# Where an expert's second layer stands, and how its first-layer weights are cut, in a mixture-of-experts stage on one core

## The chip, the cores and the metric

The kernel runs on one core of one Trainium2 chip. The metric is the time of one execution in microseconds (us). Engines are named as in the profile: PE is TensorE (PEld its weight loads), DVE is VectorE, ACT is ScalarE, POOL is GpSimd, SP is SyncE, which here issues the weight transfers.

## The reference

One transformer layer over 1024 tokens of width 1024: a latent attention, an RWKV mixer, and then a mixture of 32 experts of which each token takes 4. All but the last part ends at 967 us of the span and is not touched. What matters here is, for every expert e over the tokens that chose it:

```python
u = clamped_swiglu(h[idx] @ w1[e] + b1[e])    # w1[e]: 1024 x 2048, gate and linear columns interleaved
y[idx] += (u @ w2[e] + b2[e]) * gate          # w2[e]: 1024 x 1024
```

with `clamped_swiglu(hh) = g * sigmoid(1.702 g) * (l + 1)`, where g is the gate half limited to at most 7 and l the linear half limited to ±7. All tensors are float32. After the last expert the sum is added to the residual and normalized.

## The kernel before

The experts are taken by rank of their token count; a rank has a fixed number of places (`CAP`). 21 ranks have 128 places (called thin here) and 11 have 136 to 192 (wide). `order()` mixes them: thin, wide, thin, wide, and from there on thin, thin, wide, up to a thin one at the end.

**Precision.** Every float32 product is made of fp32r matmuls. `piece()` (L1378) loads 1 MB of weights (128 partitions x 2048) into a tile `w` (5 buffers), and splits it into a high part `wsh` (L205, a cast on ACT) and a rest `wsl` (L206, a subtraction on DVE), in two halves of 1024 columns each; the split pieces have 4 buffers (`SBUF`). Tokens are split in the same way: `xTh`, `xTl` for a thin expert, `xw` for a wide one (high and low side by side), and `uTh`, `uTl` for the second layer's input. `mm()` (L189) then issues three matmuls, high x high (L193), and the two mixed ones (L194, L195).

**An expert.** Eight pieces of w1 go into the first layer, four of w2 into the second.

- A thin expert's first layer, `first()` (L1462): four PSUM accumulators `acc` of 128 x 512, each of two pieces; a piece holds all 1024 rows (8 blocks of 128, `k`) and 256 columns, so a matmul writes 256 columns. After each accumulator come one ACT and three DVE instructions (L1483 to L1487), which give 256 columns of `u`; `flip()` (L1367) turns them with PE transposes and splits them to `uT`. The last quarter of `uT` is made by `late()`, which is called inside the second layer.
- A wide expert's first layer, `first_wide()` (L1509): weights are the stationary operand, the tokens stream past, and piece j gives the accumulators of gate and linear columns j. Each j is followed by L1535 to L1546 on ACT and DVE.
- The second layer, `second()` (L1413): for a wide expert the places over 128 are a second slot with matmuls of its own (L1435, L1439) on the same pieces, two pieces at a time. It ends with `y` (L1451 to L1455, DVE) and a scatter that adds `y` to DRAM (L1459, POOL).
- Between these, `load_x()` turns and splits the next expert's tokens, and `ahead()` makes the list of places and the gather for the expert after that (L1326 to L1362).

**Order.** The program is written expert by expert: first layer, tokens of the next, places of the one after, second layer. A scheduler then sets each engine's order by a modelled timeline and priorities, so instructions of neighbouring steps are interleaved; on the chip each engine runs its list in that order and waits by semaphores.

Of the kernel before, what the change touches and what calls it, by code (L numbers as in the profile page):

```python
# [19 lines left out]
P = 128  # L20
# [3 lines left out]
KD = D // P  # L24
# [3 lines left out]
NE = 32  # L28
# [73 lines left out]
def prep(a):  # L102

    f = lambda n: np.asarray(a[n])
    o = {}
    inv = (np.float32(10000.0) ** (-np.arange(0, 32, 2, dtype=np.float32) / np.float32(32))).astype(np.float32)
    invf = np.tile(np.repeat(inv, 2), 4).reshape(P, 1)
    sgn = np.tile(np.array([-1.0, 1.0], np.float32), 64).reshape(P, 1)
    o["vec"] = np.concatenate(
        [_cols(f("c")), _cols(f("emb_ln_g")), _cols(f("emb_ln_b")), _cols(f("ada_b")[0, :2048]),  # L110
         _cols(f("q_norm_g")), _cols(f("kv_norm_g")), _cols(f("mla_out_g")), _cols(f("rwkv_mu")),
         _cols(f("rwkv_k_k")), _cols(f("rwkv_k_a")), _cols(f("rwkv_r_k")), _cols(f("rwkv_gn_g")),
         _cols(f("rwkv_gn_b")), _cols(f("rwkv_a0")), _cols(f("ln1_g")), _cols(f("ln1_b")), invf, sgn], axis=1)
    o["cst"] = consts()
    o["thr"] = (np.array(CAP)[None, :] + P * np.arange(NB)[:, None]).astype(np.float32)[None]
    o["x"] = f("x")[0]
    o["pos"] = f("positions")
    aw = f("ada_w")[0]
    o["ada1"] = aw[:, :2048].reshape(KD, P, 4, 512).transpose(2, 1, 0, 3)
    o["ada2"] = aw[:, 2048:].reshape(KD, P, 8, 512).transpose(2, 1, 0, 3)  # L120
    o["adab2"] = f("ada_b")[:, 2048:]
    o["rows"] = np.stack([f(n).reshape(-1) for n in ROWS])
    w = f("w_in")[0]
    swap = np.arange(32) ^ 1
    blocks = [w[:, 0:128], w[:, 128:256], w[:, 256:384],
              np.concatenate([w[:, 384:416], w[:, 384:416][:, swap], np.zeros((D, 64), w.dtype)], axis=1)]
    blocks += [w[:, 416 + 128 * i:416 + 128 * (i + 1)] for i in range(14)]
    o["w_in"] = np.stack([b.reshape(KD, P, P).transpose(1, 0, 2) for b in blocks])
    q = f("w_uq")[0].reshape(256, NH, 96)
    rope = q[:, :, 64:].reshape(256, 256)  # L130
    rsw = q[:, :, 64:][:, :, swap].reshape(256, 256)
    q = np.concatenate([q[:, :, :64].reshape(256, 512), rope, rsw], axis=1)
    o["w_uq"] = q.reshape(2, P, 1024).transpose(1, 0, 2)
    o["w_uk"] = f("w_uk")[0]
    o["w_uv"] = f("w_uv")[0]
    o["w2a"] = np.concatenate([f("rwkv_w2")[0], f("rwkv_w0")], axis=0)
    o["a2"] = f("rwkv_a2")[0]
    o["g2"] = f("rwkv_g2")[0]
    o["w_o"] = f("w_o")[0].reshape(KD, P, D).transpose(1, 0, 2)
    o["rw"] = f("router_w")[0].reshape(KD, P, NE).transpose(1, 0, 2)  # L140
    o["rb"] = f("router_b")

    w1 = f("exp_w1")[0].reshape(NE, KD, P, 8, P, 2)
    o["w1"] = w1.transpose(0, 3, 2, 1, 5, 4).reshape(NE, 8, P, KD, 256)
    o["w2"] = f("exp_w2")[0].reshape(NE, 4, 2, P, D).transpose(0, 1, 3, 2, 4)
    b1 = f("exp_b1")[0].reshape(NE, 8, P, 2).transpose(0, 1, 3, 2)

    o["b1r"] = np.concatenate([b1.reshape(NE, 4, 512)] * 2, axis=1)
    o["b2"] = f("exp_b2")[0]
    o["b1c"] = b1.reshape(NE, 16, P).transpose(0, 2, 1)  # L150
    return {k: np.ascontiguousarray(v) for k, v in o.items()}
# [12 lines left out]
class Build:  # L164
# [1297 lines left out]
    def first(self, e, xT):  # L1462

        nc, mp, pm = self.nc, self.mo, self.pm
        V, S, G = nc.vector, nc.scalar, nc.gpsimd
        w1 = self.i["w1"]
        bs = self.biases(e)
        u = mp.tile([P, D], F32, name="u")
        uT = self.split_tile(mp, [P, KD, P], "uT")
        for q in range(4):  # L1470
            acc = pm.tile([P, 512], F32, name="acc", bufs=4)
            nc.tensor.matmul(acc, self.pick[:, q:q + 1].to_broadcast([P, P]), bs, start=True, stop=False)
            for j in range(2):
                ws = self.piece(w1[bass.ds(e, 1), 2 * q + j].rearrange("o p k n -> (o p) (k n)"))
                for k in range(KD):
                    w, c = ws[k // 4], k % 4 * 256
                    self.mm(acc[:, j * 256:(j + 1) * 256], xT[:, k], w[:, c:c + 256],
                            start=False, stop=(j == 1 and k == KD - 1))
            with self.tc.high_priority():
                a = acc.rearrange("p (j g f) -> p j g f", j=2, g=2)  # L1480
                v2 = lambda t: t.rearrange("p (j f) -> p j f", j=2)
                sg = mp.tile([P, 256], F32, name="sg")
                S.activation(v2(sg), a[:, :, 0], AF.Sigmoid, scale=1.702)  # L1483
                ln = mp.tile([P, 256], F32, name="ln")
                V.tensor_scalar(v2(ln), a[:, :, 1], 8.0, -6.0, ALU.min, ALU.max)
                V.scalar_tensor_tensor(v2(ln), a[:, :, 0], 7.0, v2(ln), ALU.min, ALU.mult)
                V.scalar_tensor_tensor(u[:, q * 256:(q + 1) * 256], sg, SIG7, ln, ALU.min, ALU.mult)  # L1487
                if q:
                    self.flip(uT, u, 2 * q - 2, 2 * q)

        def late():
            with self.tc.high_priority():
                self.flip(uT, u, 6, 8)
        return [uT], late
# [14 lines left out]
    def first_wide(self, e, xw, slots):  # L1509

        nc, mp, pm = self.nc, self.mo, self.pm
        V, S, G = nc.vector, nc.scalar, nc.gpsimd
        cap = xw.shape[3]
        bc = mp.tile([P, 16], F32, name="bc")
        nc.sync.dma_start(bc, self.i["b1c"][bass.ds(e, 1)].rearrange("o p n -> (o p) n"))
        lin = bc.rearrange("p (j g) -> p j g", g=2)[:, :, 1]
        G.tensor_scalar(lin, lin, 1.0, None, ALU.add)
        u0 = self.split_tile(mp, [P, KD, P], "uT")
        u1 = self.u1
        n1 = cap - P  # L1520
        w1 = self.i["w1"]
        for j in range(KD):
            ws = self.piece(w1[bass.ds(e, 1), j].rearrange("o p k n -> (o p) (k n)"))
            parts = []
            for g in range(2):
                acc = pm.tile([P, 512], F32, name="acc", bufs=4)
                for k in range(KD):
                    w = ws[k // 4]
                    c = slice(k % 4 * 256 + g * P, k % 4 * 256 + (g + 1) * P)
                    nc.tensor.matmul(acc[:, 0:2 * cap], w.hi[:, c], xw[:, k].rearrange("p a t -> p (a t)"),  # L1530
                                     start=(k == 0), stop=False)
                    nc.tensor.matmul(acc[:, 0:cap], w.lo[:, c], xw[:, k, 0], start=False, stop=(k == KD - 1))  # L1532
                with self.tc.high_priority():
                    t = mp.tile([P, cap], F32, name=f"t{g}")
                    S.activation(t, acc[:, cap:2 * cap], AF.Identity, bias=bc[:, 2 * j + g:2 * j + g + 1])  # L1535
                    V.tensor_tensor(t, acc[:, 0:cap], t, ALU.add)  # L1536
                    parts.append(t)
            with self.tc.high_priority():
                gl, ln = parts
                sg = mp.tile([P, 256], F32, name="sg")[:, 0:cap]  # L1540
                S.activation(sg, gl, AF.Sigmoid, scale=1.702)
                V.tensor_scalar(ln, ln, 8.0, -6.0, ALU.min, ALU.max)
                V.scalar_tensor_tensor(ln, gl, 7.0, ln, ALU.min, ALU.mult)
                V.scalar_tensor_tensor(ln, sg, SIG7, ln, ALU.min, ALU.mult)
                self.split(u0[:, j], ln[:, 0:P])
                self.split(Split(u1[:, j, 0, 0:n1], u1[:, j, 1, 0:n1]), ln[:, P:cap])  # L1546
        return [u0, u1], None
# [84 lines left out]
    def moe(self):  # L1632
# [11 lines left out]
        slots, rows, x = {}, {}, {}  # L1644
# [7 lines left out]
        ahead(0)  # L1652
        x[0] = self.load_x(rows[0])
        ahead(1)
        for i, r in enumerate(order):
            e = nc.values_load(self.eid[0:1, r:r + 1], engines=[mybir.EngineType.SP], skip_runtime_bounds_check_because=ok)
            uT, late = self.first(e, x[i]) if len(slots[i]) == 1 else self.first_wide(e, x[i], slots[i])
            if i + 1 < NE:
                x[i + 1] = self.load_x(rows[i + 1])
            ahead(i + 2)  # L1660
            self.second(e, slots[i], uT, late, i == NE - 1)

    def overflow(self):

# [144 lines left out]
```

## Time and profile before

| | |
|---|---|
| time, median of 3 runs | 2460.11 us (2459.35 to 2463.05) |
| the profiled execution: its time / its span | 2454.54 us / 2452.8 us |
| busy over the span: PE, DVE, ACT, POOL | 2280.2, 2003.6, 1409.0, 562.3 us |
| expert stage, from about 967 to 2400 us: its length / DVE busy / ACT busy | 1433.0 / 1297.42 / 970.52 us |
| weights loaded in it | 384 pieces of 1024 KB |

A matmul's busy time in the trace is longer than the time until the next one can start, since matmuls are pipelined; what a matmul takes of PE is read from start to start. PE's granted clock is a share of full speed (1.00 is 2.4 GHz, 0.50 is 1.2 GHz).

### The profile page before, as it was taken

The numbers are of one execution on the slowest core, as the hardware profiler recorded it, in microseconds if no ns is written. First come the engines' busy times: TensorE is split into PE (matmuls) and PEld (weight loads), VectorE is DVE, ScalarE is ACT, GpSimd is POOL, SyncE is SP. The second block draws the span as 40 slices with busy tenths as digits, with TensorE's granted clock in tenths as the row PEclk, the third lists the DMA queues.
The fourth block names the chain that finished last, engine by engine and source line by source line (L and its number), as shares of the span: only waits on it lengthen the run. The fifth ranks groups of instructions, "written<-read, shape, count | busy, mean of one in ns | idle before, by whom it ended". The sixth has DMA issues, their size and how long they took to land. (4 is left out here: it accounts for less than half of the span.)

```text
span 2452.8 us, 42049 instructions
## 1 busy us (share of the span) xinstructions
PE 2280.2 (93%) x15539; PEld 1934.8 (79%) x15539; DVE 2003.6 (82%) x3878; ACT 1409.0 (57%) x2355; POOL 562.3 (23%) x411
## 2 busy tenths in 40 slices
PE   6999989999998995999999999999999999999992
PEld 3776766776665784889898998989999898888881
DVE  7666447778786776789898989898989899898977
ACT  5323325455555433667676767676767676666764
POOL 1004223222213433111111312121312121221113
PEclk9999989999999996899999999999999999999996
DMA  6377542222123323878798989797989898898973
GB/s 269 119 257 275 199 113 56 58 46 58 33 42 85 113 94 140 313 282 311 290 341 297 329 288 348 276 356 275 350 287 343 308 327 321 297 330 301 325 271 138
DMA packets 167334, 567.80 MB, mean 231 GB/s; under 512 B 64616, under 2 KB 79737, under 8 KB 116820
## 3 DMA queue, kind: packets, MB, share of 16 engines
q1 hardware_dynamic: 155476, 524.63, 58.6%
q0 software_dynamic: 11216, 39.34, 6.5%
q8 instruction: 124, 2.03, 0.3%
q10 hardware_dynamic: 432, 1.09, 0.1%
q14 instruction: 86, 0.70, 0.1%
HBM read 508.22 MB, written 56.79 MB: 230 GB/s over the span
## 5 line engine op out<-in xcount | busy, mean ns | idle before, releaser
L206 DVE TENSOR_TENSOR wsl<-w,wsh 128x1024 fp32r<-128x1024 f32 x786 | 935.9, 1224 | 138.4 <-ACT wsh L205 136.9
L205 ACT CAST wsh<-w 128x1024 fp32r<-128x1024 f32 x786 | 782.8, 1047 | 345.2 <-PE acc L195 91.1
L193 PE MATMUL acc<-wsh,xTh 128*128 128x256 f32 x1344 | 382.4, 286 | 9.9 <-ACT xTh L205 6.2
L194 PE MATMUL acc<-wsl,xTh 128*128 128x256 f32 x1344 | 383.3, 286 | 0.7 <-DVE wsl L206 0.7
L1530 PE MATMUL acc<-xw,wsh 128*128 128x368 f32 (+7 forms) x1408 | 376.8, 351 | 6.0 <-DVE t L1536 6.0
L195 PE MATMUL acc<-wsh,xTl 128*128 128x256 f32 x1344 | 382.1, 285 | 0.3 <-DVE xTl L206 0.3
L1532 PE MATMUL acc<-xw,wsl 128*128 128x184 f32 (+7 forms) x1408 | 335.9, 239 | 0.0
L1530 PEld LDWEIGHTS acc<-xw,wsh 128*128 128x128 f32 x1408 | 265.9, 189 | 7.9 <-issue 3.2
L1532 PEld LDWEIGHTS acc<-xw,wsl 128*128 128x128 f32 x1408 | 270.3, 192 | 0.7
L193 PEld LDWEIGHTS acc<-wsh,xTh 128*128 128x128 f32 x1344 | 258.9, 193 | 13.3 <-ACT xTh L205 8.4
L194 PEld LDWEIGHTS acc<-wsl,xTh 128*128 128x128 f32 x1344 | 259.8, 193 | 4.8 <-DVE wsl L206 1.0
L195 PEld LDWEIGHTS acc<-wsh,xTl 128*128 128x128 f32 x1344 | 259.6, 193 | 1.7 <-DVE xTl L206 0.6
L1459 POOL DMA_INDIRECT y_d<-y,idx x42 | 148.4, 3532 | 403.2 <-DVE y L1451 318.6
L1362 POOL DMA_INDIRECT xg<-h_d,idx x43 | 99.1, 2305 | 614.7 <-issue 267.8
L193 PE MATMUL acc<-wsh,uTh 128*128 128x512 f32 x512 | 203.3, 400 | 18.0 <-ACT uTh L205 18.0
L194 PE MATMUL acc<-wsl,uTh 128*128 128x512 f32 x512 | 202.4, 396 | 0.0
L195 PE MATMUL acc<-wsh,uTl 128*128 128x512 f32 x512 | 192.7, 404 | 1.2 <-DVE uTl L206 1.2
L193 PEld LDWEIGHTS acc<-wsh,uTh 128*128 128x128 f32 x512 | 97.4, 190 | 39.9 <-ACT uTh L205 20.8
L193 PE MATMUL sm<-hTh,wsh 128*128 128x512 f32 x288 | 116.2, 404 | 7.2 <-DVE stage L445 2.2
L194 PE MATMUL sm<-hTl,wsh 128*128 128x512 f32 x288 | 116.9, 406 | 4.2 <-DVE hTl L347 3.1
L195 PE MATMUL sm<-hTh,wsl 128*128 128x512 f32 x288 | 114.9, 399 | 0.0
L194 PEld LDWEIGHTS acc<-wsl,uTh 128*128 128x128 f32 x512 | 97.6, 191 | 19.2
(584 smaller groups left out, 4337.2 us busy)
## 6 DMA issues: line engine op xcount, KB each, us to landing
w<-in_w_dram SPq DMA_DIRECT2D x384, 1024.0 KB
aw<-in_ada_dram SPq DMA_DIRECT2D x34, 512.0 KB
w<-in_w_in_dram SPq DMA_DIRECT2D x18, 512.0 KB
aw<-in_ada_dram SPq DMA_DIRECT2D x7, 1024.0 KB
rkv_d<-stage SPq DMA_DIRECT2D x12, 512.0 KB
xt<-in_x_dram SPq DMA_DIRECT2D x8, 512.0 KB
xr<-in_x_dram SPq DMA_DIRECT2D x8, 512.0 KB
xr_d<-xr SPq DMA_DIRECT2D x8, 512.0 KB
```

Of the source, the lines that this page charges most:

```text
L193: mm(out, a.hi, b.hi, start=start, stop=False)
L194: mm(out, a.hi, b.lo, start=False, stop=False)
L195: mm(out, a.lo, b.hi, start=False, stop=stop)
L205: (hi_eng or self.nc.scalar.copy)(dst.hi, src)
L206: (lo_eng or self.nc.vector).tensor_tensor(dst.lo, src, dst.hi.bitcast(F32), ALU.subtract)
L1362: self.nc.gpsimd.indirect_dma_start(out=xg[0:n], out_offset=None, in_=self.h2_d, in_offset=bass.IndirectOffsetOnAxis(ap=idx[0:n, 0:1], axi ...
L1459: nc.gpsimd.indirect_dma_start(out=self.y_d, out_offset=bass.IndirectOffsetOnAxis(ap=idx[0:n, 0:1], axis=0), in_=y[0:n], in_offset=None, c ...
L1530: nc.tensor.matmul(acc[:, 0:2 * cap], w.hi[:, c], xw[:, k].rearrange("p a t -> p (a t)"), start=(k == 0), stop=False)
L1532: nc.tensor.matmul(acc[:, 0:cap], w.lo[:, c], xw[:, k, 0], start=False, stop=(k == KD - 1))
```

## The change

The host's layout of w1 is cut differently: a piece now holds 512 rows (4 blocks k) and 512 columns instead of 1024 rows and 256 columns. It is as large as before, and there are as many. In `first()` the two pieces of an accumulator are two halves of the rows, and a matmul writes all 512 columns. In `first_wide()` two pieces are loaded at every even j and serve j and j + 1. In `moe()` the second layer of an expert is issued after the next expert's first layer; for the last expert the one before it is finished first. `late` of the newer expert is handed to the older one's second layer, where a wide expert calls it once in each of its two slots.

```diff
-    w1 = f("exp_w1")[0].reshape(NE, KD, P, 8, P, 2)
-    o["w1"] = w1.transpose(0, 3, 2, 1, 5, 4).reshape(NE, 8, P, KD, 256)
+    w1 = f("exp_w1")[0].reshape(NE, 2, 4, P, 4, 2, P, 2)
+    o["w1"] = w1.transpose(0, 4, 1, 3, 2, 5, 7, 6).reshape(NE, 8, P, 4, 512)
...
-            for j in range(2):
-                ws = self.piece(w1[bass.ds(e, 1), 2 * q + j].rearrange("o p k n -> (o p) (k n)"))
-                for k in range(KD):
-                    w, c = ws[k // 4], k % 4 * 256
-                    self.mm(acc[:, j * 256:(j + 1) * 256], xT[:, k], w[:, c:c + 256],
-                            start=False, stop=(j == 1 and k == KD - 1))
+            for m in range(2):
+                ws = self.piece(w1[bass.ds(e, 1), 2 * q + m].rearrange("o p k n -> (o p) (k n)"))
+                for k in range(4):
+                    c = k % 2 * 512
+                    self.mm(acc, xT[:, 4 * m + k], ws[k // 2][:, c:c + 512], start=False, stop=(m == 1 and k == 3))
...
-            ws = self.piece(w1[bass.ds(e, 1), j].rearrange("o p k n -> (o p) (k n)"))
+            if j % 2 == 0:
+                ws = []
+                for m in range(2):
+                    ws += self.piece(w1[bass.ds(e, 1), j + m].rearrange("o p k n -> (o p) (k n)"))
...
+        due = None
         for i, r in enumerate(order):
+            last = i == NE - 1
+            if last:
+                self.second(*due, None)
             e = nc.values_load(...)
             uT, late = self.first(e, x[i]) if len(slots[i]) == 1 else self.first_wide(e, x[i], slots[i])
-            if i + 1 < NE:
+            if not last:
                 x[i + 1] = self.load_x(rows[i + 1])
-            ahead(i + 2)
-            self.second(e, slots[i], uT, late, i == NE - 1)
+                ahead(i + 2)
+                if due:
+                    self.second(*due, late)
+                elif late:
+                    late()
+            due = e, slots[i], uT
+        self.second(*due, late, True)
```

PE before, at the end of a thin expert's second layer (`uT`) ahead of the wide expert with 176 places, whose first layer reads `xw`:

```order
L1374 MATMUL tr<-csts,u 128x128 x2
L1374 MATMUL tr<-csts,xg 128x128 x8
L1374 MATMUL tr<-csts,xg 128x48 x4
L195 MATMUL acc<-wsh,uTl 128x512 x2
L193 MATMUL acc<-wsh,uTh 128x512
L194 MATMUL acc<-wsl,uTh 128x512
L195 MATMUL acc<-wsh,uTl 128x512
L193 MATMUL acc<-wsh,uTh 128x512
```

PE of the change at the same place; what follows is the rest of the 8 matmuls of L1330, two more transposes of `u`, and then the wide expert's first matmul:

```order
L193 MATMUL acc<-wsh,uTh 128x512 x2
L194 MATMUL acc<-wsl,uTh 128x512
L195 MATMUL acc<-wsh,uTl 128x512
L194 MATMUL acc<-wsl,uTh 128x512
L195 MATMUL acc<-wsh,uTl 128x512
L1374 MATMUL tr<-csts,u 128x128 x2
L1374 MATMUL tr<-csts,xg 128x128 x8
L1374 MATMUL tr<-csts,xg 128x48 x8
L1330 LDWEIGHTS oh
```

Before, some 20 matmuls of the second layer stand behind the first transposes of the wide expert's tokens (`xg`); in the change all of the second layer stands ahead of all 16. This is so at nine of the eleven wide experts, and at the first one with a first layer in place of the second.

DVE before, at the same expert, from the last thin-expert work to the split of `xw`:

```order
L206 TENSOR_TENSOR wsl<-w,wsh 128x1024 x2
L206 TENSOR_TENSOR uTl<-tr,uTh 128x256
L1486 SCALAR_TENSOR_TENSOR ln<-acc,ln 128x256
L206 TENSOR_TENSOR xw<-tr,xw 128x4x128 x2
L206 TENSOR_TENSOR xw<-tr,xw 128x4x48
L1487 SCALAR_TENSOR_TENSOR u<-sg,ln 128x256
L206 TENSOR_TENSOR wsl<-w,wsh 128x1024 x2
L206 TENSOR_TENSOR xw<-tr,xw 128x4x48
```

DVE of the change, at the same place:

```order
L1451 SCALAR_TENSOR_TENSOR y<-acc,gate,g2p 128x512 x2
L206 TENSOR_TENSOR wsl<-w,wsh 128x1024
L1486 SCALAR_TENSOR_TENSOR u<-sg,ln 128x256
L206 TENSOR_TENSOR wsl<-w,wsh 128x1024
L206 TENSOR_TENSOR uTl<-tr,uTh 128x256
L206 TENSOR_TENSOR xw<-tr,xw 128x4x128 x2
L206 TENSOR_TENSOR xw<-tr,xw 128x4x48
L1338 TENSOR_SCALAR at<-tr,csts 128x1
```

Before, `y` of the thin expert (L1451) stands 14 rows behind the first split of `xw`; in the change it stands ahead of it, with two halves of a weight piece, `u` and `uTl` between them.

## Rows read from the trace of the kernel before

**Rows 1.** Windows: start:end, us, busy us (instructions) by engine, PEclk, DMA share, GB/s.

```profile
1317.00:1448.70 131.70, 130.61 (x906) 120.32 (x905) 122.56 (x195) 90.39 (x139) 28.87 (x9) 1.00 0.87 314
```

**Rows 2.** Windows of its parts: thin first, second; thin first, second, rest; wide.

```profile
1317.00:1340.90 23.90, 23.90 (x198) 23.75 (x197) 23.90 (x30) 18.24 (x23) 7.00 (x1) 1.00 0.94 333
1340.90:1352.90 12.00, 11.37 (x70) 9.19 (x69) 12.00 (x19) 7.77 (x11) 0.00 (x0) 1.00 0.95 382
1352.90:1379.30 26.40, 26.40 (x209) 25.76 (x208) 25.74 (x35) 19.41 (x23) 12.07 (x3) 1.00 0.86 303
1379.30:1391.00 11.70, 11.24 (x66) 8.66 (x65) 11.70 (x17) 8.27 (x14) 3.30 (x1) 1.00 1.01 422
1391.00:1398.40 7.40, 7.40 (x53) 6.92 (x50) 6.66 (x12) 5.21 (x8) 1.05 (x1) 1.00 0.89 337
1398.40:1430.00 31.60, 31.60 (x242) 31.58 (x240) 29.36 (x63) 22.05 (x46) 2.50 (x1) 1.00 0.87 287
1430.00:1448.70 18.70, 18.70 (x88) 14.45 (x85) 13.21 (x24) 9.44 (x16) 2.95 (x2) 1.00 0.62 229
```

**Rows 3.** Waits of PE, 960 to 2390 us: us in total, times, longest.

```profile
PE acc L193 <- ACT uTh L205: 10.4, 9, 2.3
PE acc L193 <- ACT xTh L205: 6.2, 10, 0.6
PE acc L1530 <- DVE t L1536: 6.0, 7, 1.5
```

**Rows 4.** Waits of DVE and ACT in the same stretch.

```profile
DVE wsl L206 <- ACT wsh L205: 107.8, 99, 5.2
ACT wsh L205 <- PE acc L195: 91.1, 100, 2.1
ACT wsh L205 <- DMA w<-in_w_dram: 24.9, 14, 5.7
```

**Rows 5.** Groups by form: one of three equal lines of the thin first layer.

```profile
L193 PE MATMUL acc<-wsh,xTh 128*128 128x256 f32 x1344 | 382.4, 286 | 9.9 <-ACT xTh L205 6.2 <-ACT wsh L205 3.7
```

**Rows 6.** Timeline of PE, first into second layer: start, us, instruction [idle before].

```profile
1378.74 0.28 PE L194 MATMUL acc<-wsl,xTh 128*128 128x256 f32 x1
1379.22 0.28 PE L195 MATMUL acc<-wsh,xTl 128*128 128x256 f32 x1
...
1380.72 0.39 PE L193 MATMUL acc<-wsh,uTh 128*128 128x512 f32 x1
...
1382.09 0.38 PE L1374 MATMUL tr<-csts,u 128*128 128x128 f32 x2
1382.93 0.50 PE L193 MATMUL acc<-wsh,uTh 128*128 128x512 f32 x1 [0.46 <-ACT uTh L205]
```

**Rows 7.** Timeline of PE: twelve transposes of tokens and what follows.

```profile
1017.96 1.43 PE L1374 MATMUL tr<-csts,xg 128*128 128x128 f32 x12
1019.31 0.50 PE L194 MATMUL acc<-wsl,uTh 128*128 128x512 f32 x1
```

**Rows 8.** Timeline of DVE around a thin expert's output `y`.

```profile
1363.84 1.22 DVE L206 TENSOR_TENSOR wsl<-w,wsh 128x1024 fp32r<-128x1024 f32 x1
1364.97 1.41 DVE L1451 SCALAR_TENSOR_TENSOR y<-acc,gate,g2p 128x512 f32<-128x512 f32 x2
1366.29 2.35 DVE L206 TENSOR_TENSOR wsl<-w,wsh 128x1024 fp32r<-128x1024 f32 x2
1368.56 0.42 DVE L1487 SCALAR_TENSOR_TENSOR u<-sg,ln 128x256 f32<-128x256 f32 x1
1368.89 1.23 DVE L206 TENSOR_TENSOR wsl<-w,wsh 128x1024 fp32r<-128x1024 f32 x1
```

**Rows 9.** Groups of DVE by form, 1317 to 1448.7 us.

```profile
L206 DVE TENSOR_TENSOR uTl<-tr,uTh 128x256 fp32r<-128x256 f32 x8 | 3.4, 422 | 0.0
L206 DVE TENSOR_TENSOR xw<-tr,xw 128x512 fp32r<-128x512 f32 x2 | 1.3, 696 | 0.0
L206 DVE TENSOR_TENSOR xw<-tr,xw 128x192 fp32r<-128x192 f32 x2 | 0.7, 360 | 0.0
```

**Rows 10.** Timeline of DVE in a wide second layer.

```profile
1440.52 4.63 DVE L206 TENSOR_TENSOR wsl<-w,wsh 128x1024 fp32r<-128x1024 f32 x4 [3.49 <-ACT wsh L205]
1447.87 2.36 DVE L206 TENSOR_TENSOR wsl<-w,wsh 128x1024 fp32r<-128x1024 f32 x2 [1.40 <-ACT wsh L205]
```

More of the change, by code (lines that the diff above doesn't have):

```diff
@@ L1526, in first_wide @@
                 acc = pm.tile([P, 512], F32, name="acc", bufs=4)
+                a = j % 2 * 2 + g
                 for k in range(KD):
-                    w = ws[k // 4]
-                    c = slice(k % 4 * 256 + g * P, k % 4 * 256 + (g + 1) * P)
+                    w, c = ws[k // 2], slice(k % 2 * 512 + a * P, k % 2 * 512 + (a + 1) * P)
                     nc.tensor.matmul(acc[:, 0:2 * cap], w.hi[:, c], xw[:, k].rearrange("p a t -> p (a t)"),
```

## The prediction

> **What bounds the kernel now.** I read the windows of the expert stage first, then the waits of PE, DVE and ACT, then the timelines for what one instruction really takes. One round of the steady pattern thin, thin, wide is 131.7 us, and in it PE is busy for 130.6, DVE for 122.6, ACT for 90.4 [rows 1]. So PE sets the pace and DVE is 9.1 us behind it, with ACT and the DMA engines (0.87 of their time) further off. The parts of the round [rows 2] show that this is two different limits: over both thin experts, 1317.0 to 1391.0 us, DVE is busy for 73.3 of 74.0 us while PE is nearly full too, and the whole slack of DVE lies with the wide expert: 0.7 + 2.2 + 5.5 us in the last three windows. What ends DVE's idle time is the cast on ACT, 107.8 us in all, and what ends the waits of that cast is mostly PE letting a split buffer go (91.1 us for one of the matmul lines; weights that had not landed: 24.9 us) [rows 4]. DVE is thus held by PE's use of the four split buffers, and PE itself hardly waits: its waits for data in the steady stretch are 10.4, 6.2 and 6.0 us over the whole of it [rows 3]. What the change takes from PE counts, as far as DVE can follow.
>
> **Part 1: wider matmuls in the thin first layer.** There are 3 x 1344 matmuls of 256 columns, so 192 for each of 21 thin experts [rows 5]; 96 of 512 columns take their place. From start to start a 256-column matmul takes 0.48/4 = 0.120 us, a 512-column one of the second layer (1.37 us for six) 0.228 us [rows 6]. 192 x 0.120 = 23.04 us becomes 96 x 0.228 = 21.89 us: 1.15 us less for each thin expert, 24 us for 21. With the reading accuracy of those starts, 0.226 to 0.230, it is 20 to 28. PE's clock is at 1.00 through all of this [rows 1], so it gives nothing more. Pieces have the same bytes, number and order of arrival, so loading is unchanged; splitting too.
>
> Here a rule speaks against the change. The rows show that a matmul takes 13 ns (256 columns) and 15 ns (512) beyond its columns at 2.4 GHz: 120 against 106.7 ns, 228 against 213.3 [rows 6]. The Trainium skill, "TensorE: Matmul & The Clock Gate", section "Wait — 56ns, not 53.3ns?", gives a warm matmul its columns at 2.4 GHz plus some 2.5 ns; by that, an estimate from its figures, the halved count would save 0.25 us of a thin expert and 5 us in all instead of 24. The trace disagrees with it for these two shapes, and the sum goes by the trace.
>
> **Part 2: the second layer one expert later.** The 10.4 us that PE waits for `uTh` (9 times) stand where the second layer starts on its own expert's last quarter of `u`; rows 6 show one, with the two transposes of `u`, then 0.46 us idle, ahead of the next matmul. A first layer now lies between, so they go: -10.4. The 6.2 us for `xTh` (10 times) are at the start of a thin first layer [rows 3]; in the new order those transposes stand among the wide expert's second-layer matmuls, so I count -6.2. Bounds: from none of these to all, 0 to -16.6; I take all, since no PE instruction behind them needs the result within a microsecond.
>
> `late` runs twice in the second layer of ten wide experts: two transposes (0.24 us by the rate in rows 7), one cast and one `uTl` of 0.42 us [rows 9] too many. On PE that is +2.4 us; on DVE 4.2 us over the stage, hidden under its slack of 9.1 us a round, or added if that is gone.
>
> **Part 3: a new wait, which the order shows.** At nine wide experts all 16 transposes of `xw` now follow the whole second layer of the thin expert, and nothing but 4 transposes of `u` and 8 very short matmuls stands between them and the wide expert's first matmul, which needs `xw` split. On DVE that split is queued behind `y`, and `y` cannot start until the second layer's last matmul has ended. So from that end DVE does: `y`, 1.32 us; two halves of a piece, 2.27; `u`, 0.33, all from start to start [rows 8]; `uTl` 0.42; three splits of `xw`, 0.70 + 0.70 + 0.36 [rows 9]: 6.10 us. In this time PE has its 20 transposes, (1.35/12) x 20 = 2.25 us [rows 7]. It waits 3.85 us, nine times: +35 us. Queued behind the waiting matmul is the whole wide first layer, and DVE's sums `t` wait for it. Before, some 20 matmuls of 0.228 us, 4.6 us, covered that chain. From below: if DVE had only the splits left, 1.76 us and the cast ahead of the first, the transposes would cover it, 0; nearest to the order is 2 us as a low case, since `y` alone must come after. From above: DVE is busy without a pause in the thin experts [rows 2], so it can reach `y` late by the two halves queued ahead of it, 2.3 us more: 6.2 us each, +56. I take 3.85.
>
> **Part 4: pieces in pairs in the wide first layer.** Two pieces now serve j and j + 1 and go free together, so two of four split buffers are in use rather than one. What this does is seen where pairs are used already, in the wide second layer: DVE stops there for 3.49 and 1.40 us until a pair goes free [rows 10], with no wait of PE for it. The wide first layer has DVE at 29.4 of 31.6 us [rows 2], so PE could wait there by the second half of a pair. Against that, the pause of part 3 lets DVE get ahead at the very start of it, and the 6.0 us for `acc` [rows 3] may go. I count -4, between -6 and +20 (half of such a 3.5 us stop at each of 11 experts).
>
> **Sum.** -24 - 16.6 + 2.4 + 35 - 4 = -7.2 us on the profiled execution's 2454.5, so 2447.3. That execution was 5.6 us below the median of the three runs, 2460.1; set against the median the forecast is **2453 us**. Startup, until the clock and the transfers are up, and the last expert, whose second layer still follows its own first layer, are left as they are.
>
> **The rivals.**
> - *DVE comes late (slower).* Place: `y` ahead of `xw` at the end of the thin pair. PE gets through two thin experts 2.3 us sooner, DVE does not: it was busy for 73.3 of 74.0 us there. If it reaches `y` more than about 1 us after the second layer's end, the pause is 5 to 6.2 us and eats all gains: nine times 2.3 more is +21, so 2474. For: rows 2. Against: DVE's slack of 7.7 us in the wide expert can be spent as a lead of two to three pieces before the thin ones.
> - *The pause is short (clearly faster).* If DVE and ACT serve `xw` early enough that PE waits 2 us rather than 3.85, the sum gains 17 us: 2436. For: 20 transposes and the casts run in that time anyway. Against: the fixed order on DVE.
> - *The columns cost what they cost (slower).* If the 512-column matmuls in a stream of alternating weights save only 0.25 us of an expert, 19 us of part 1 are missing: 2472. Against: both durations are measured in this trace, among the same kind of weight loads. This is the skill's rule above.
> - That the change does not do what it says is no case: the order shows both parts.
>
> **How the numbers follow.** Forecast, 2442 to 2462: 0.42. Short pause, around 2436: 0.23. DVE late, 2462 to 2485: 0.27. The page's rule: 0.03. Anything else, slower for the most part: 0.05. 0.2% of the time, about what a measurement of this kernel can tell from no change, is 4.9 us: 2455.2 to 2465.0. Of the forecast's 0.42 some 0.25 lies below that and 0.17 within; with the short pause, faster is 0.48; the lower end of the late DVE gives the rest of the same, 0.22; slower 0.30. Eight times in ten it should lie between 2432 and 2478: the low end is the short pause with part 1 at 28 us, the high end the late DVE with a little for the pairs. The likeliest case's own range is 2442 to 2462.
>
> **What would show it.** Right: the three matmul lines of the thin first layer count 672 each, at 512 columns, 0.228 us apart; the wait of the second layer for `uTh` is gone but for the last expert; and PE has a new wait for `xw`, nine or ten times, around 4 us each, released by DVE's split. A round is then within 1 us of 131.7. Wrong: no such wait (then it is clearly faster), or one of over 5 us with DVE busy ahead of it (then slower), or new waits of PE for `wsh` or `wsl` of the second piece of a pair inside the wide first layer.

## The result, and the profile after

| | before | after |
|---|---|---|
| time, median of 6 runs each | 2460.12 us (2451.47 to 2463.05) | 2485.07 us (2476.01 to 2492.52) |
| ratio | | 1.0113, 95% interval 1.009 to 1.0135 |
| profiled execution: its time / its span | 2454.54 / 2452.8 us | 2482.1 / 2480.3 us |

The change makes the kernel 1.1% slower. To compare kernels I use one stretch throughout: from the first matmul of the second wide expert to that of the tenth, eight rounds of thin, thin, wide. In the windows view (columns as in [rows 1]) it is, in the kernel before,

```profile
1124.20:2178.10 1053.90, 1036.72 (x7235) 953.67 (x7234) 972.69 (x1555) 723.46 (x1105) 219.24 (x72) 1.00 0.87 314
```

and in the changed kernel,

```profile
1116.80:2193.20 1076.40, 1029.97 (x5713) 888.14 (x5712) 977.67 (x1572) 733.61 (x1119) 265.85 (x73) 0.97 0.84 310
```

Here lie 22.5 of the 27.5 us by which the span grew. PE is busy for 6.8 us less and idle for 29 us more, and its mean clock fell from 1.00 to 0.97: the stretches recorded at 1.2 GHz sum up to 56 us in these rounds, 3 before. DVE's busy time hardly moved. The next table divides a round of PE's time by what it runs, each matmul counted from its start to the next start, and idle times over 0.15 us taken out. The last three columns are experiments told below.

| us in a round | before | after | cut alone (e1) | cut alone, DVE lighter (e12) | after, tokens earlier (e11) |
|---|---|---|---|---|---|
| thin first layers | 46.44 | 43.76 | 44.08 | 44.24 | 43.79 |
| wide first layer | 33.90 | 35.31 | 33.78 | 33.74 | 34.78 |
| second layers | 41.36 | 41.31 | 42.96 | 41.07 | 40.86 |
| transposes, places, biases | 7.89 | 8.43 | 8.26 | 7.46 | 8.36 |
| idle | 2.15 | 5.74 | 5.03 | 0.08 | 1.70 |
| sum | 131.74 | 134.55 | 134.11 | 126.58 | 129.49 |
| at 1.2 GHz | 0.4 | 7.0 | 3.4 | 0.0 | 1.7 |

The thin first layers got shorter as forecast; idle time and a longer wide first layer took that back twice over. The new matmuls, by form (line, shape, count, busy us, mean ns), where [rows 5] had 1344 of 256 columns:

```profile
L193 PE MATMUL acc<-wsh,xTh 128*128 128x512 f32 x672 | 262.0, 394 | 6.4 <-ACT wsh L205 5.6 <-ACT xTh L205 0.7
```

What PE waits for in the changed kernel, over the stretch of [rows 3] (us in total, times, longest):

```profile
PE tr L1374 <- DVE uTl L206: 41.8, 9, 4.9
PE tr L1374 <- DVE u L1486: 9.3, 5, 7.1
PE tr L1374 <- DVE xw L206: 2.5, 9, 0.6
PE acc L1533 <- DVE xw L206: 2.2, 1, 2.2
PE acc L193 <- ACT xTh L205: 0.7, 1, 0.7
```

The waits for `uTh` are gone, those for `xTh` nearly so. New is a wait of a transpose (L1374), 51.1 us in all. Nine idle times of 4.75 to 7.11 us stand ahead of nine wide experts. This is the one at 2054 us, on PE (start, us, instruction, idle before):

```profile
2052.14 0.39 PE L195 MATMUL acc<-wsh,uTl 128*128 128x512 f32 x1
2052.84 0.44 PE L1374 MATMUL tr<-csts,u 128*128 128x128 f32 x2 [0.30 <-DVE u L1486]
2053.11 1.39 PE L1374 MATMUL tr<-csts,xg 128*128 128x128 f32 x12
2059.36 0.60 PE L1374 MATMUL tr<-csts,xg 16*128 16x16 f32 x4 [4.87 <-DVE uTl L206]
2059.96 0.35 PE L1330 MATMUL tr<-td,oh 128*128 128x6 bf16 x8
2060.56 0.69 PE L1374 MATMUL tr<-csts,u 128*128 128x128 f32 x2 [0.25 <-DVE xw L206]
2060.90 0.59 PE L1533 MATMUL acc<-xw,wsh 128*128 128x288 f32 x1
2061.28 0.32 PE L1535 MATMUL acc<-xw,wsl 128*128 128x144 f32 x1
2061.40 0.53 PE L1533 MATMUL acc<-xw,wsh 128*128 128x288 f32 x1
```

and on DVE:

```profile
2052.71 2.34 DVE L206 TENSOR_TENSOR wsl<-w,wsh 128x1024 fp32r<-128x1024 f32 x2
2054.98 1.39 DVE L1451 SCALAR_TENSOR_TENSOR y<-acc,gate,g2p 128x512 f32<-128x512 f32 x2
2056.30 2.34 DVE L206 TENSOR_TENSOR wsl<-w,wsh 128x1024 fp32r<-128x1024 f32 x2
2058.57 0.41 DVE L1486 SCALAR_TENSOR_TENSOR u<-sg,ln 128x256 f32<-128x256 f32 x1
2058.90 0.41 DVE L206 TENSOR_TENSOR uTl<-tr,uTh 128x256 fp32r<-128x256 f32 x1
2059.24 1.53 DVE L206 TENSOR_TENSOR xw<-tr,xw 128x512 fp32r<-128x512 f32 x4
```

Read them together. The second layer's last matmul starts at 2052.14. PE turns two blocks of `u` and three groups of `xw` tokens; these four results fill the four `tr` buffers. The fourth group of four transposes needs a buffer back, and the oldest is let go by `uTl` on DVE. `uTl` stands behind two halves of weights, `y`, two more halves and `u`: DVE reaches `y` only 2.8 us after that last matmul began (2.0 to 2.9 at the nine), since it is late itself. The buffer settles where PE waits, but hardly how long: DVE is through with `xw` at 2060.77, 0.13 us ahead of the wide expert's first matmul.

A stop of DVE itself shows 47 us earlier:

```profile
2007.21 0.42 DVE L206 TENSOR_TENSOR uTl<-tr,uTh 128x256 fp32r<-128x256 f32 x1 [3.64 <-ACT uTh L205]
```

DVE stands for 3.64 us, since the cast to `uTh` waits for two transposes of `u` (its third quarter), and these stand in PE's order among the matmuls of the wide expert's second layer. From there to `y` DVE has no pause over 0.22 us. Such a stop of DVE, of 3.64 to 4.90 us, comes ahead of each of the nine stops of PE; from 960 to 2390 us DVE waits 40.3 us for `uTh`, 6.5 in the kernel before. It is longer than the time by which DVE is late at `y`. Whether DVE would be in time without it, no run tells by itself.

PE stands for 4.87 us, and the clock falls to half within it and stays there behind it. In the stretch around another of these stops, at 1386 us,

```profile
1386.10:1392.90 6.80, 4.81 (x28) 4.63 (x29) 5.29 (x12) 0.69 (x2) 3.89 (x2) 0.50 0.91 310
```

the granted clock is 0.50, and PE is busy for 4.81 of the 6.80 us. A pair of wide matmuls takes 0.50 us behind the stop shown above (2060.90 to 2061.40), against 0.24 at full clock (in e11, below).

### The profile page after: what moved, and what is told of

Same layout as the page of the kernel before. It is cut to its first block, busy times and chain, and to the rows that moved or that the text cites. A ratio compares the mean times of both kernels' runs of the same rounds, so it can differ in the third digit from the quotient of the medians.

```text
span 2480.3 us, 38054 instructions
## 1 busy us (share of the span) xinstructions
PE 2275.0 (92%) x13543; PEld 1850.6 (75%) x13543; DVE 1992.6 (80%) x3888; ACT 1416.5 (57%) x2365; POOL 631.4 (25%) x411
## 5 line engine op out<-in xcount | busy, mean ns | idle before, releaser
L206 DVE TENSOR_TENSOR wsl<-w,wsh 128x1024 fp32r<-128x1024 f32 x786 | 926.4, 1218 | 73.9 <-ACT wsh L205 73.7
L1533 PE MATMUL acc<-xw,wsh 128*128 128x368 f32 (+7 forms) x1408 | 392.1, 363 | 2.2 <-DVE xw L206 2.2
L1459 POOL DMA_INDIRECT y_d<-y,idx x42 | 207.2, 4932 | 466.4 <-DVE y L1451 343.2
L1533 PEld LDWEIGHTS acc<-xw,wsh 128*128 128x128 f32 x1408 | 278.0, 198 | 2.7 <-DVE xw L206 2.5
L194 PE MATMUL acc<-wsl,xTh 128*128 128x512 f32 x672 | 265.7, 395 | 3.2 <-DVE wsl L206 3.2
L193 PE MATMUL acc<-wsh,xTh 128*128 128x512 f32 x672 | 262.0, 394 | 6.4 <-ACT wsh L205 5.6
L195 PE MATMUL acc<-wsh,xTl 128*128 128x512 f32 x672 | 264.0, 393 | 0.0
L1362 POOL DMA_INDIRECT xg<-h_d,idx x43 | 78.3, 1821 | 566.6 <-PE acc L1535 178.2
L193 PE MATMUL acc<-wsh,uTh 128*128 128x512 f32 x512 | 184.5, 401 | 6.3 <-ACT uTh L205 6.1
L193 PEld LDWEIGHTS acc<-wsh,xTh 128*128 128x128 f32 x672 | 127.8, 190 | 33.7 <-ACT wsh L205 5.9
L194 PEld LDWEIGHTS acc<-wsl,xTh 128*128 128x128 f32 x672 | 127.8, 190 | 31.0 <-DVE wsl L206 4.1
L195 PEld LDWEIGHTS acc<-wsh,xTl 128*128 128x128 f32 x672 | 127.6, 190 | 27.0 <-DVE xTl L206 0.2
L1538 ACT ACTIVATE t<-acc,bc 128x152 f32<-128x152 f32 (+7 forms) x176 | 65.4, 394 | 96.5 <-PE acc L1535 84.1
```

The lines of the kernel that those rows point to most:

```text
L193: mm(out, a.hi, b.hi, start=start, stop=False)
L194: mm(out, a.hi, b.lo, start=False, stop=False)
L195: mm(out, a.lo, b.hi, start=False, stop=stop)
L206: (lo_eng or self.nc.vector).tensor_tensor(dst.lo, src, dst.hi.bitcast(F32), ALU.subtract)
L1362: self.nc.gpsimd.indirect_dma_start(out=xg[0:n], out_offset=None, in_=self.h2_d, in_offset=bass.IndirectOffsetOnAxis(ap=idx[0:n, 0:1], axi ...
L1459: nc.gpsimd.indirect_dma_start(out=self.y_d, out_offset=bass.IndirectOffsetOnAxis(ap=idx[0:n, 0:1], axis=0), in_=y[0:n], in_offset=None, c ...
```

## The experiments

All times are medians; ratios are against runs of the kernel before on the same chip, with 95% intervals. "Cut" is the new shape of the pieces, "shift" the second layer one expert later. Theory A says that the stops ahead of the wide experts, and the clock behind them, are the loss (A', for short, that these come of the order of the `tr` buffers, whatever DVE's load); B, that pieces taken in pairs are; C, that DVE is too late whatever PE saves. Rows of waits below are of 1115 to 2330 us. Few of the forecasts came out: by the time alone B's in e1, the second of e4, C's in e10, that of A' in e11 and the second of e14; every other range was missed. So the theories are judged by the waits and the rounds, and not by the time alone.

**e1: the cut alone.** The loop of before with the new pieces:

```diff
-            due = e, slots[i], uT
-        self.second(*due, late, True)
+            ahead(i + 2)
+            self.second(e, slots[i], uT, late, i == NE - 1)
```

> The new cut of the first-layer weights alone, with the second layer where the kernel before has it. Theory A (the loss is the stop of PE ahead of a wide expert and the low clock behind it, both made by the shift): faster than before by 15 to 25 us, 2435 to 2445; the 512-column matmuls keep their pitch of 0.227, no stop of 5 us ahead of the wide experts, the uTh waits of about 20 us stay, and half-clock time in the expert stage stays near 27 us. Theory B (taking two pieces at a time in a wide first layer costs): slower than before, 2465 or more, with waits of PE for wsh or wsl at line 1533. Theory C (VectorE sets the pace, whatever PE saves): within 5 us of 2460.

Measured: 2475.82 us, ratio 1.0085 (1.0056 to 1.0115). Theory A's forecast is refuted: the cut alone loses, with no shift and no stop of 5 us. The time lies in B's range, and C's (within 5 us of 2460) is missed as well. PE waits in the thin second layers for what DVE and ACT make of `u`; at 2012 us the timeline reads

```profile
2008.89 0.69 PE L1374 MATMUL tr<-csts,u 128*128 128x128 f32 x4
2011.45 0.50 PE L193 MATMUL acc<-wsh,uTh 128*128 128x512 f32 x1 [1.87 <-ACT uTh L205]
...
2014.35 1.22 PE L195 MATMUL acc<-wsh,uTl 128*128 128x512 f32 x2 [1.70 <-DVE uTl L206]
```

In all there are 46 us of it, with no wait for `wsh` or `wsl` at L1533, which B asked for, so B has only its time:

```profile
PE acc L193 <- ACT uTh L205: 20.4, 17, 1.9
PE acc L195 <- DVE uTl L206: 11.8, 9, 1.7
PE tr L1330 <- DVE uTl L206: 10.6, 9, 1.2
PE tr L1374 <- DVE uTl L206: 3.6, 10, 0.4
```

**e2: the shift alone.** The new loop with the pieces of before.

> The second layer one expert later alone, with the first-layer pieces of before (1024 rows by 256 columns). Theory A: the nine or ten stops of about 5 us (some 52 us) and some 70 us more at half clock (worth some 34) come, less the 17 us of waits that the shift removes: slower than before by 50 to 75 us, 2510 to 2535. Theory B (the pieces taken in pairs cost): no slower than before, 2440 to 2460. Theory C (VectorE sets the pace): within 10 us of the changed kernel's 2485.

Measured: 2503.67 us, ratio 1.019 (1.0151 to 1.0228). The stops are there:

```profile
PE tr L1374 <- DVE uTl L206: 15.9, 5, 4.0
PE tr L1374 <- DVE u L1487: 14.3, 3, 5.9
```

Each half of the change loses by itself, 21 and 49 us over the kernel before on that chip (2454.83), and together they lose less than the shift alone. The 2503.67 lies in no theory's range; A's is nearest.

**e3: tokens a whole first layer earlier.**

```diff
+            if i and not last:
+                x[i + 1] = self.load_x(rows[i + 1])
...
             uT, late = self.first(e, x[i]) if len(slots[i]) == 1 else self.first_wide(e, x[i], slots[i])
```

> The changed kernel with one statement moved: the tokens of the next expert are transposed and split (load_x) ahead of the current expert's first layer, so that xw is there long before the wide expert begins. Theory A: the stop ahead of each wide expert goes (9 times about 5.5 us, 50 us) and with it the half-clock stretches behind it (some 69 us of them, worth 34): 2400 to 2425. Theory B (pairs of pieces): the stops go but PE waits for wsh or wsl in wide experts: 2455 to 2480. Theory C (VectorE sets the pace, 122 us busy in a round of 135): the stop turns up elsewhere, 2440 to 2460.

Measured: 2487.15 us, ratio 1.0136 (1.0089 to 1.0183). The stop turned up elsewhere: the tokens had not landed (PE waits 34.5 us for `xg` in ten times, 8.4 at most). So the run says nothing on the stop's price; e11 mends it.

**e4: PE kept busy in the stop.** Ahead of the fourth group of `xw`:

```diff
+                for k in range(40 if q == 0 else 0):
+                    self.nc.tensor.transpose(pt[:, 256 + k % 2 * P:384 + k % 2 * P], rows[0][:, k % 8 * P:k % 8 * P + P],
+                                             self.ident)
```

> The changed kernel with 40 needless transposes (128 by 128, about 0.117 us each, 4.7 us in all) put on PE into the unused half of a PSUM buffer at the place where it stops ahead of a wide expert, so that the stop stays as long as it is but PE isn't idle in it. If the low clock comes of PE standing still there: half-clock time in the expert stage falls from about 96 us to about 30, and the time by some 30 us, to 2450 to 2460, with the round near 131. If the low clock has another cause (load, not the stop): no half-clock time saved, 2480 to 2495.

Measured: 2483.25 us, ratio 1.0105 (1.0062 to 1.0148). The place now reads

```profile
2063.69 4.59 PE L1515 MATMUL tr<-csts,xg 128*128 128x128 f32 x40
2068.63 0.42 PE L1512 MATMUL tr<-csts,xg 16*128 16x16 f32 x4 [0.35 <-DVE uTl L206]
```

and the time at 1.2 GHz in the eight rounds went from 56 to 17 us: the low clock does come of the standing PE. Of the nine rounds to the eleventh wide expert seven have every stop filled and nothing at 1.2 GHz. Their mean is 131.65 us, against 133.64 for the same rounds of the changed kernel with 7.3 us each at 1.2 GHz: 2.0 us a round is what the clock costs. The whole time didn't fall: in the other two rounds PE stops for `u` first (8.8 and 7.1 us, from 1249 and 1792 us), the needless transposes come behind that stop, and these rounds are 9.6 and 3.6 us longer than in the changed kernel, which has the second of these stops too. My 2450 to 2460 was a miss.

The Trainium skill, "TensorE: Matmul & The Clock Gate", section "Terms", prices throttled time at one minus the share of clock granted, so at half of it. By that rule, as an estimate from it, the 7.3 us a round would cost 3.7. The runs show 2.0, less than the rule's. PE is idle in 2.0 of the 7.3 us, which explains a part of the difference.

**e5 and e6: the cut for thin experts only**, the weights lying in memory in both shapes; e5 with the loop of before, e6 with the new one.

```diff
-        w1 = self.i["w1"]
+        w1 = self.i["w1w"]
...
+            ws = self.piece(w1[bass.ds(e, 1), j].rearrange("o p k n -> (o p) (k n)"))
```

> The loop of before; the first-layer weights lie in memory in both cuts, thin experts take pieces of 512 rows by 512 columns, wide ones those of 1024 by 256 as before, so that no pieces are taken in pairs. Theory B (the pairs let VectorE run only two pieces ahead in the wide first layer, and what it doesn't do there it lacks later): faster than the 2476 of the pieces alone and than before, 2430 to 2445. Theory C (VectorE's 122 us of work in a round set the pace, and whatever PE saves in thin experts comes back as waits for u or for split pieces): 2452 to 2470.

> The changed kernel with wide experts taking pieces of 1024 rows by 256 columns (weights in memory in both cuts): the shift and the thin cut without the pairs. Theory B (pairs): VectorE's idle time in the wide first layer (6.5 us in a round of the changed kernel) shrinks to some 2 and the time falls by 20 to 40, to 2445 to 2465. Theory A (the stop by the order of the tr buffers): the stop stays, 2478 to 2490. Theory C: within 10 of 2485 too, VectorE's busy time 122 us a round and its idle time 12.

Measured: e5 2491.88 us, ratio 1.0129 (1.008 to 1.0177); e6 2498.16 us, 1.0141 (1.0099 to 1.0183). Both miss all their ranges. Without pairs neither kernel is faster than with them, so theory B has nothing for it, here or in the waits of e1. That e5 is slower than e1 is not explained; the order on each engine is planned anew for every kernel.

**e7 and e8: GpSimd takes two low half splits of each thin expert**, in the changed kernel and in the one before.

```diff
-            self.split(ws[:, slice(*c)], w[:, slice(*c)])
+            self.split(ws[:, slice(*c)], w[:, slice(*c)], lo_eng=nc.gpsimd if pool and c[0] else None)
```

> The changed kernel with two of the 24 half splits of the low part (128 by 1024, 1.13 us each on VectorE) of each thin expert done by GpSimd instead. This takes 21 x 2 x 1.13 = 47 us of VectorE's work away and none of PE's. Theory C (VectorE sets the pace): faster by 30 to 47, 2438 to 2455, VectorE's busy time in a round 117.5 instead of 122. Theory A or B alone (the stop ahead of wide experts, the pairs): it shortens the stop by the VectorE work ahead of it at most, 10 to 20 us, 2465 to 2475.

> The kernel before with the same two half splits of each thin expert on GpSimd. Theory C: faster by 20 to 47 than before, 2410 to 2435. If PE sets the pace in the kernel before, as the prediction had it (PE busy 130.6 of 131.7 us): only the 24 us of PE's waits for uTh, xTh and t can go, 2436 at best, and 2450 is likelier; slower if GpSimd's splits (2.6 to 3.9 us each, behind a scatter) come late.

Measured: e7 2476.04 us, ratio 1.0052 (1.0023 to 1.0081); e8 2506.09 us, 1.0165 (1.0123 to 1.0208). Neither is in a range. Inconclusive for C, as DVE's work did not shrink: its busy time in the eight rounds rose from 977.7 to 994.9 us in e7. The timeline shows why, on GpSimd

```profile
2105.28 2.41 POOL L206 TENSOR_TENSOR wsl<-w,wsh 128x1024 fp32r<-128x1024 f32 x1 [19.14 <-DVE t L1546]
2113.74 2.69 POOL L206 TENSOR_TENSOR wsl<-w,wsh 128x1024 fp32r<-128x1024 f32 x1 [3.47 <-ACT wsh L205]
```

and on DVE in the same time:

```profile
2105.80 2.97 DVE L206 TENSOR_TENSOR wsl<-w,wsh 128x1024 fp32r<-128x1024 f32 x1
2114.41 3.10 DVE L206 TENSOR_TENSOR wsl<-w,wsh 128x1024 fp32r<-128x1024 f32 x1
2118.55 1.22 DVE L206 TENSOR_TENSOR wsl<-w,wsh 128x1024 fp32r<-128x1024 f32 x1
```

A split on DVE takes 1.22 us by itself and about 3 beside one on GpSimd; both times it ends 1.08 us after GpSimd's. The Trainium skill, "GPSIMD Engine Reference", section "Key points", says that the two engines share SBUF interfaces and contend where a DVE instruction has two SBUF inputs, as this subtraction has; the trace agrees.

**e9, e10 and e12: a part of DVE's work left out.** Two low half splits of each thin expert are left out (PE reads another half's low part, so the output differs): e9 in the changed kernel, e10 in the one before, e12 in the cut alone.

```diff
+            if cut and c[0]:
+                nc.scalar.copy(ws.hi[:, slice(*c)], w[:, slice(*c)])
+            else:
+                self.split(ws[:, slice(*c)], w[:, slice(*c)])
+        return ws[:, 0:1024], Split(ws.hi[:, 1024:2048], ws.lo[:, 0:1024]) if cut else ws[:, 1024:2048]
```

> The changed kernel, in which two of the 24 low half splits of each thin expert are left out (PE reads another half's low part in their place, so the output differs); no engine gets other work for it. 4.5 us of VectorE's work in a round go, 47 us in all, and none of PE's. Theory C (VectorE's work and the waits that hang on it set the pace): VectorE busy about 117.5 us in a round, the stop ahead of wide experts shortens or goes, 2438 to 2455. Theory A' (the stop comes of the order of the tr buffers, whatever VectorE's load): the stop keeps over 4 us of its 4.9, 2475 to 2485.

> The kernel before with the same two low half splits of each thin expert left out (the output differs). Theory C: the 16.7 us of waits for uTh and more go, 2415 to 2440. If PE sets the pace in the kernel before and VectorE doesn't: 2445 to 2462, since PE's 130.6 us of a round's 131.7 stay.

> The new cut alone (loop of before) with two of the 24 low half splits of each thin expert left out (the output differs). If the new cut alone is slow because VectorE comes late with u and its split parts in thin experts, whose PE work got shorter: its waits for uTh, uTl and in the slots' place (44 us) shrink to under 15, a round takes 129 to 130, and the time is 2410 to 2435. If it is slow for another reason (pairs, order of the instructions): a round stays over 132.5, 2455 to 2475.

Measured: e9 2428.15 us, ratio 0.9884 (0.985 to 0.9918); e10 2436.41 us, 0.991 (0.9883 to 0.9937); e12 2401.37 us, 0.9775 (0.9753 to 0.9797). The same 47 us of DVE's work are worth 57 us in the changed kernel, 74 in the cut alone, and some 20 in the kernel before. That puts e10 into C's range, but only 2.8 of its 20 us lie in its eight rounds (1051.10 us), and most of the rest behind the tenth wide expert; PE's time without idle is 129.9 us a round there, against 129.6. e9 and e12 came out below their ranges. In e12 the eight rounds are

```profile
1130.10:2142.70 1012.60, 1011.87 (x5698) 869.90 (x5696) 934.66 (x1521) 725.04 (x1105) 170.78 (x72) 1.00 0.87 326
```

with PE busy throughout, its clock at 1.00, and as its only wait 0.9 us for `uTl`. PE needs 126.5 us for a round of the new cut, if DVE is in time.

The place where DVE's work binds is the thin pair, from its first matmul to the wide expert's. The mean of the eight pairs (windows view):

| us in a thin pair | before | before, DVE lighter (e10) | cut alone (e1) | cut alone, DVE lighter (e12) |
|---|---|---|---|---|
| length | 75.0 | 74.1 | 77.7 | 70.3 |
| DVE busy | 73.6 | 70.0 | 73.7 | 69.2 |

Two single pairs, that of the waits of e1 shown above and the same one in e12:

```profile
1986.40:2064.90 78.50, 72.44 (x349) 58.34 (x347) 73.88 (x99) 53.37 (x71) 12.45 (x6) 0.98 0.91 341
1948.40:2018.50 70.10, 70.10 (x349) 57.30 (x347) 69.42 (x95) 53.76 (x71) 21.16 (x6) 1.00 0.96 370
```

In the kernel before PE set the pace of a round and DVE was just fast enough. With the cut PE could be through a pair in 70.3 us, and DVE's 73.7 us of work do not fit in that: as long as all of it lies there, the cut can win little over 1 us a pair. This much of theory C is shown. That e1 is slower than before it does not explain: DVE is idle for 4.0 us of its pair, 2.7 of them soon behind the waits shown (up to 2018.99 us), and in front of the awaited `uTl` it had four halves of weights to split. That speaks for the order there, and not for DVE's load; no run tests it.

Nor do these runs take away DVE's work alone, since with less of it the order came out otherwise. In e9 DVE's splits of `xw` no longer stand behind `y`:

```profile
2019.52 1.41 DVE L206 TENSOR_TENSOR xw<-tr,xw 128x512 fp32r<-128x512 f32 x3
2024.61 0.74 DVE L1454 SCALAR_TENSOR_TENSOR y<-acc,gate,g2p 128x512 f32<-128x512 f32 x1
```

Twelve transposes of the tokens stand ahead of the second layer's last 30 matmuls there, and DVE's own stop for `uTh` is gone from the eight rounds. The stops of PE are almost gone (what is left is 6.5 us for `xw` in eight times and 11.5 for the gather), but whether by the lighter DVE or by the order e9 can't tell.

**e11: tokens in the middle of the first layer.** The changed kernel, with no work taken from any engine:

```diff
+            if q == 2:
+                mid()
...
+            def mid():
+                if not last:
+                    x[i + 1] = self.load_x(rows[i + 1])
```

(and the same at j = 4 of a wide expert; the call behind the first layer goes).

> The changed kernel with load_x of the next expert called in the middle of the current expert's first layer: early enough that the wide expert's transposes have the second layer to hide behind, late enough that the gathered tokens are there. No work is taken from any engine. Theory A' (order): the stops of 4.9 us and the half clock behind them go, and no wait for the gather as in the run with the tokens a whole first layer earlier: 2410 to 2440, faster than the kernel before. Theory C (VectorE sets the pace): the stops turn up as waits for u, t or split pieces, 2450 to 2480, VectorE busy 122 us in a round.

Measured: 2437.4 us, ratio 0.9924 (0.9896 to 0.9951), six runs. It beats both kernels. The start of the tenth wide expert, which has 144 places like the ninth, shown above, now reads

```profile
2127.11 1.38 PE L1374 MATMUL tr<-csts,xg 128*128 128x128 f32 x12
...
2137.94 0.35 PE L1374 MATMUL tr<-csts,xg 16*128 16x16 f32 x3
2138.22 0.44 PE L1374 MATMUL tr<-csts,u 128*128 128x128 f32 x2
2138.59 0.23 PE L1374 MATMUL tr<-csts,xg 16*128 16x16 f32 x1
...
2139.77 0.34 PE L1537 MATMUL acc<-xw,wsh 128*128 128x288 f32 x1
2139.95 0.23 PE L1539 MATMUL acc<-xw,wsl 128*128 128x144 f32 x1
2140.01 0.34 PE L1537 MATMUL acc<-xw,wsh 128*128 128x288 f32 x1
```

Twelve transposes come 12 us ahead of the wide expert's first matmul (2139.57), 44 matmuls of the second layer stand between, and PE does not stop. Over the eight rounds

```profile
1103.70:2139.60 1035.90, 1022.29 (x5702) 882.00 (x5701) 968.90 (x1559) 728.50 (x1114) 284.46 (x72) 0.99 0.87 320
```

DVE has all its work (968.9 us) and is idle for 67 us instead of 99; its stop for `uTh` is gone from these rounds. So the order by itself, as theory A' had it, can remove the stops; it is worth 48 us here, against the 57 of e9.

**e13 and e14.** e13 is e11 with the pieces of before; e14 is e11 with `ahead(i + 2)` called in `mid()` too.

> The shift alone (cut of before) with load_x in the middle of the first layer. If the stop ahead of the wide experts was what made the shift alone 49 us slower: no stop of over 3 us, rounds near 131, 2440 to 2460, and the run with both halves of the change and load_x in the middle (2437) is faster by PE's 2.3 us a round, up to 20. If VectorE sets the pace even so: within 5 us of 2437.

> As the run e11 (load_x in the middle), with the gather of the expert after next issued there too, ahead of the first layer's second half. If e11's remaining waits for the gather (13.5 us in 1115 to 2330) cost what they show: 2420 to 2432. If the earlier slot computation only moves VectorE's work ahead of u and the splits: 2437 or slower.

Measured: e13 2478.88 us, ratio 1.0108 (1.0079 to 1.0137); e14 2465.54 us, 1.0031 (1.0011 to 1.0051). e13 missed its range: 25 us came back of the shift's 49, but the shift with the old pieces still loses. In this order the cut is worth some 41 us (e13 against e11), with all of DVE's work. The waits left in e13 are mostly the gather's:

```profile
PE tr L1374 <- DMA xg<-h_d,idx: 24.6, 7, 7.7
```

e14 answers the other way than hoped: the gather's waits stay (13.5 us in e11), and one for `y` joins them.

```profile
PE acc L1537 <- DVE y L1451: 14.6, 10, 2.3
PE tr L1374 <- DMA xg<-h_d,idx: 14.6, 5, 6.0
```

## Why the prediction was wrong

Forecast 2453 us, 2432 to 2478; it is 2485.

- **Part 3 is the step that failed: its term was mis-sized.** Its place was right, nine wide experts, and so was the chain on DVE: 5.79 us from the start of `y` to the end of `xw` (2054.98 to 2060.77), where I had 6.10. What was wrong is when it begins. I let `y` start as the second layer's last matmul ends; DVE comes to it 2.8 us after that matmul's start, with two halves ahead of it, as the rival of the late DVE had it. I had 3.85 us for each; the stops are 4.75 to 7.11, and in all 55.8 us of new waits (51.1 + 2.5 + 2.2) instead of 35. That is the upper bound that part 3 had itself, 56. I also let all 20 transposes run beside that chain, when the fourth group waits for a `tr` buffer that only `uTl` gives back; this moved the wait, as said above, more than it lengthened it.
- **PE's clock was left out.** It falls to half in each stop. The wide first layer takes 35.31 us a round against 33.90, the transposes and the rest 0.5 more (with the second run of `late`); e4 prices the clock at 2.0 us a round, so some 18 for nine.
- **Part 1 was right as PE's own time.** 1.15 us less was forecast for each thin expert, 1.34 measured (2.68 a round), from 512-column matmuls 0.227 us apart. The Trainium skill's rule, the rival of chance 0.03, is out. But the prediction said that the saving counts "as far as DVE can follow", and the sum then ignored it: [rows 2] had DVE busy for 73.3 of 74.0 us in the thin pair, and the table of the thin pair shows that DVE's work does not fit into the time that PE needs with the cut.
- **Part 2 was right for PE.** Of 10.4 and 6.2 us of waits 0.7 are left. What it did not see is that in the new order DVE waits for `uTh`, 40.3 us in place of 6.5.
- **Part 4** was within its error: pairs cost nothing that the runs show. The -4 did not come either.

With the measured sizes: -28 (21 x 1.34) - 16 + 56 + 18 = +30, and the span grew by 27.5. The rival "DVE comes late" was the true one, at 2474 for want of the clock; "wrong if one of over 5 us with DVE busy ahead of it" is what the trace shows in kind, with 4.75 to 4.87 us at eight of the nine. The chances gave it 0.27 where the row of the thin pair spoke for more.

What stays open: how much of DVE's lateness at `y` is its load and how much its own stop for `uTh`, since e9 and e11 have neither the stops nor the old order; why the cut alone loses, and not only fails to win; why the shift with the old pieces loses even in e13, and why e5 is slower than e1. No run tells these apart from the new order that each kernel gets.

## What to carry to other kernels

Where two engines are within a few per cent of each other over a stage, read each part of the stage by itself: work taken from the one counts only where the other has room, and here the room lay with the wide experts, not with the thin ones that were made shorter, until the order was changed once more (e11). Before moving a step, look at what its first instructions must have (a rotating buffer as well as data) and who gives that back; look for new waits of the second engine too, and not only of the first; and count for a stop of several microseconds on TensorE both the stop and the slower clock behind it. The same change with one call moved (e11) is 1.9% faster than without (2437.4 against 2485.07 us).

## What the runs showed of the hardware

- A 128x1024 subtraction on VectorE with both inputs in SBUF took 2.97 and 3.10 us while GpSimd did one of its own, 1.22 us alone (e7), and both times it ended 1.08 us after GpSimd's. Giving GpSimd 32 splits in eight rounds (two for each thin expert) raised VectorE's busy time by 17 us instead of taking 36 (32 x 1.13) from it.
- Around two short waits of TensorE of 1.87 and 1.70 us, with 1.2 us of matmuls between them, the clock fell to half as well (0.50 from 2013.9 to 2017.3 us in e1, within the second wait). e1 has 27 us of half clock in its eight rounds without a single stop of 2 us there: a kernel can lose clock without a long stop.
